# A residual stream kept with tokens on partitions, with down and output projections whose stationary operand is the activations

## The chip, the core and the metric

The kernel runs on one core of one Trainium2 chip. The metric is device time in microseconds (us) from the first to the last instruction of the program, with what lies around it; less is better. The time before is 2877.26 us, the median of two runs (2877.17 and 2877.34).

## What is computed

Two layers over 256 tokens of width 2048, in float32. Each layer adds to x half of a gated feed forward (FFN, inner width 4096), then a mixer, then half of a second FFN. The mixer of layer 0 is a gated delta net with pooling (GDN), that of layer 1 a latent attention (MLA) with 16 heads.

```
def swiglu(h, w_gate, w_up, w_down):
    return (jax.nn.silu(h @ w_gate) * (h @ w_up)) @ w_down
...
    for layer in range(DEPTH):
        x = x + 0.5 * swiglu(rms_norm(x, ffn1_norm[layer]), ...)
        h = rms_norm(x, mix_norm[layer])
        x = x + delta_pool_mixer(h, ...)  or  mla_mixer(h, ...)
        x = x + 0.5 * swiglu(rms_norm(x, ffn2_norm[layer]), ...)
```

So there are six norms, four down projections (4096 to 2048) and two output projections (2048 to 2048), `wgo` in GDN and `wmo` in MLA.

## The kernel before

**Precision.** Every large product is made from float32r parts. A weight piece of 1024 columns is split by `piece` (L163 to L169): ACT writes the rounded part `whi`, DVE writes the rest `wlo`. An activation tile is split in the same way into [128, 2, 256]: high part, then low part. Three of the four part products are kept: whi with high, whi with low, wlo with high.

**Layout.** x lies with features on partitions: 16 tiles of 128 features by 256 tokens. All large products have the weights as stationary side (128 x 128, loaded into the array) and the activations as moving side. In `mm3` the wide form is one product of whi with [high | low], 512 columns, and one of wlo with high, 256 columns, both into one PSUM bank of 128 features by 512. The narrow form (GDN's and MLA's input projections) is three products of 256 columns.

**Down projection.** For each of 16 feature tiles d: 32 K tiles of `g`, two products each; then DVE adds the two halves of the bank to x (`add_residual`, two operations of 256 columns), and `after(d)` does the norm's share for this tile: `feed_parts` splits x[d] times the gain into `xg[d]` (ACT, then DVE), `feed_squares` adds its square to `acc` (POOL, for the last two tiles ACT and DVE). Since `xg[d]` is already in the layout that the next product wants, PE has no work at the handoff. `project_out` does the same for the output projections, where the first two feature tiles share their steps so that late activations are waited for later.

**Norm factor.** After the first products of the next stage PE sums `acc` over partitions with a product of ones (`end_norm`, L321), and ACT and DVE make R, the factor of every token, from it.

**Weights.** SP loads 1 MB at a time into one of three `raw` buffers; there are four buffers each of `whi` and `wlo`. PSUM has six banks for streamed products and two for others in the FFNs, four and four in the mixers.

**Order.** Instructions are traced in the order in which PE is to run them; latency-bound chains (`Chains`) are traced in between by a clock of estimated PE time, and a scheduler places them on each engine. Each engine runs its own list in order.

**Start and end.** `warm_up` (L270) issues eight float32 products of zeros while the first loads are under way. The first gate and up tiles (`opening`) then go through K in quarters as x comes in. At the end `store` writes each feature tile of x from ACT's queue.

Of the kernel before, what the change touches and what calls it, by code (L numbers as in the profile page):

```python
# [9 lines left out]
F32 = mybir.dt.float32  # L10
# [8 lines left out]
P = 128  # L19
# [78 lines left out]
class Builder:  # L98
# [17 lines left out]
    def behind(self, inst, earlier):  # L116
        """inst issues after `earlier` on their engine."""
# [4 lines left out]
    def table(self, which, out, in_, func, **kw):  # L122
        """An activation that needs a table set; all of them issue in the order of the trace."""
# [12 lines left out]
    def banks(self, mm, aux):  # L136
        """The phase's PSUM: how many banks for the streamed products and how many for all others."""
# [10 lines left out]
    def split_hi_lo(self, dst, src, scale=None):  # L148
        """dst [P, 2, n] (float32r) = the two exact parts of src * scale."""
# [13 lines left out]
    def piece(self, raw, h):  # L163
        """The two exact parts of columns h : h + 1024 of a raw weight slab."""
# [6 lines left out]
    def weights(self, *aps):  # L171
        """Stream [P, L] weight slabs; yields (hi, lo) pieces [P, 1024]."""
# [15 lines left out]
    def gemm(self, ps, stream, acts, wide=True):  # L188
        """ps[:, :256] (+ ps[:, 256:] when wide) = W^T act over the K tiles in acts ([P, 2, 256] hi/lo)."""
# [25 lines left out]
    def squares(self, dst, src):  # L215
        """dst [P, 2, n] (float32r) = the two exact parts of src^2."""
# [6 lines left out]
    def total(self, out, which, sq):  # L223
        """out = the sums of sq over the partitions that `which` (float32r, 0 or 1) joins."""
# [3 lines left out]
    def rsqrt(self, out, ss, scale, newton, tag="rs"):  # L228
        """out = (ss * scale + EPS) ** -0.5, elementwise."""
# [18 lines left out]
    def token_major(self, r, out):  # L248
        """out [P, 2] = the row that all partitions of r [P, 256] hold, tokens on partitions."""
# [20 lines left out]
    def warm_up(self):  # L270
        """Products of zeros while the first loads are under way: TensorE's clock doubles after 3.4 us of work."""
        z = self.tmp([P, S], "res")
        self.nc.vector.memset(z, 0.0)
# [5 lines left out]
    def load_x(self, c):  # L279
        """A quarter of x and its part in the first norm."""  # L280
        t = self.xp.tile([P, 4, S], F32, tag=f"x{c}", name=f"x{c}")
        self.nc.sync.dma_start(t, self.i["x"][:, 4 * c : 4 * c + 4, :])
        self.x += [t[:, k, :] for k in range(4)]

    def load_rest(self):
        self.nc.sync.dma_start(self.ca, self.i["ca"])
        self.nc.scalar.copy(self.ones_r, self.ones)
        for d in range(KT):
            self.feed_squares(d, False)

    def begin_norm(self, gain):
        self.gain = gain
        self.xg = [None] * KT
        self.acc = self.tmp([P, S], "acc", 1)

    def feed_parts(self, d):
        """Splits x[d] * gain."""
        t = self.xp.tile([P, 2, S], F32R, tag=f"xg{d}", name=self.nm("xg"))
        self.split_hi_lo(t, self.x[d], self.gains[:, self.gain, d : d + 1])
        self.xg[d] = t  # L300

    def feed_squares(self, d, pool):
        """Adds x[d]^2 to the sum of squares."""
        nc = self.nc
        eng = nc.gpsimd if pool else nc.vector
# [819 lines left out]
```

## Time and profile before

| | before |
|---|---|
| median of the runs | 2877.26 us |
| profiled execution, span | 2874.8 us |
| PE busy | 2866.9 us, 17322 products |
| weight loads (PEld) busy | 2527.4 us |
| DVE / ACT / POOL busy | 1888.8 / 1439.9 / 200.3 us |
| DMA read | 507.74 MB |

The page gives for each engine the time in which an instruction of it was under way. PE's instructions overlap, so PE busy for the whole span does not say how fast it goes; for that one reads the distance between the starts of products in the timeline. The chain that ended last is the list of what the last instruction waited for, followed back to the start.

### The profile page before, as it was taken

How to read it: one execution, taken by the hardware profiler on the slowest of the kernel's cores; microseconds unless marked ns; L12 is line 12 of the kernel's file. 1: busy time of each engine (PE TensorE's matmuls, PEld its weight loads, DVE VectorE, ACT ScalarE, POOL GpSimd, SP SyncE). 2: the span in 40 equal slices, each digit the busy share in tenths (PEclk: the TensorE clock that was granted, in tenths of full speed). 3: DMA queues.
4: the chain of work that ended last, by engine and by line, in shares of the span. 5: the costliest groups of instructions: out<-in, count | busy, mean ns of one | idle time of the engine just before them, and what ended most of it. 6: DMA issues, size and time to landing. Idle time of an engine off the chain costs nothing.

```text
span 2874.8 us, 42334 instructions
## 1 busy us (share of the span) xinstructions
PE 2866.9 (100%) x17322; PEld 2527.4 (88%) x17322; DVE 1888.8 (66%) x2683; ACT 1439.9 (50%) x2146; POOL 200.3 (7%) x228
## 2 busy tenths in 40 slices
PE   9999999999999999999999999999999999999999
PEld 8888888899998888888888888888998888888888
DVE  7666666676787766666656666666777776666554
ACT  6444443475464544444345444544577454444433
POOL 0000011000003000001110000011122210000000
PEclk9999999999999999999999999999999999999999
DMA  6555555544245555555555555555533455555553
GB/s 247 183 188 190 183 184 189 187 147 164 88 162 191 189 183 185 190 185 183 189 190 179 188 190 185 183 189 189 183 125 112 151 185 191 185 185 187 196 195 137
DMA packets 77843, 512.70 MB, mean 178 GB/s; under 512 B 10833, under 2 KB 13649, under 8 KB 16849
## 3 DMA queue, kind: packets, MB, share of 16 engines
q1 hardware_dynamic: 74192, 506.81, 50.0%
q10 hardware_dynamic: 3456, 3.20, 0.3%
q8 instruction: 135, 2.21, 0.3%
q14 instruction: 60, 0.48, 0.1%
HBM read 507.74 MB, written 2.10 MB: 177 GB/s over the span
## 4 chain that ended last, share of the span: by engine, by line
PE 98%; issue 1%; DVE 0%; ACT 0%; POOL 0%; DMA 0%; SPq 0%; DVEq 0%; ACTq 0%; POOLq 0%
PE mm L186 93%; PE aux L186 4%; PE aux L641 0%; PE aux L957 0%; ACT whi L167 0%; DMA x<-in_x 0%; DVE wlo L168 0%; POOL osq L221 0%; PE aux L321 0%; ACT xg L155 0%; DVE y L485 0%; POOL sq L221 0%; PE aux L681 0%; DVE cb L627 0%; DVE tg L626 0%
## 5 line engine op out<-in xcount | busy, mean ns | idle before, releaser
L186 PE MATMUL mm<-xg,whi 128*128 128x512 f32 (+1 forms) x5664 | 1717.8, 367 | 0.9 <-ACT whi L167 0.9
L168 DVE TENSOR_TENSOR wlo<-raw,whi 128x1024 fp32r<-128x1024 f32 x960 | 1197.4, 1248 | 572.7 <-ACT whi L167 564.4
L167 ACT CAST whi<-raw 128x1024 fp32r<-128x1024 f32 x960 | 1007.8, 1050 | 799.8 <-PE mm L186 688.0
L186 PE MATMUL mm<-xg,wlo 128*128 128x256 f32 x4880 | 1330.2, 281 | 0.5 <-DVE wlo L168 0.5
L186 PEld LDWEIGHTS mm<-xg,whi 128*128 128x128 f32 x5664 | 997.7, 189 | 167.8 <-ACT whi L167 1.3
L186 PEld LDWEIGHTS mm<-xg,wlo 128*128 128x128 f32 x4880 | 923.2, 189 | 26.4 <-DVE wlo L168 1.0
L186 PE MATMUL mm<-g,whi 128*128 128x512 f32 x2048 | 719.1, 398 | 0.0
L186 PE MATMUL mm<-g,wlo 128*128 128x256 f32 x2048 | 564.7, 281 | 0.0
L186 PEld LDWEIGHTS mm<-g,whi 128*128 128x128 f32 x2048 | 380.8, 188 | 89.7
L186 PEld LDWEIGHTS mm<-g,wlo 128*128 128x128 f32 x2048 | 386.8, 189 | 6.0
L392 ACT COPY u<-mm 128x256 f32<-128x256 f32 x256 | 95.1, 372 | 465.4 <-PE mm L186 465.3
L393 DVE TENSOR_TENSOR t<-mm,u 128x256 f32<-128x256 f32 x256 | 108.7, 425 | 247.0 <-ACT u L392 246.9
L394 DVE TENSOR_TENSOR t<-t,R 128x256 f32<-128x256 f32 x256 | 108.6, 426 | 8.4
L312 POOL TENSOR_TENSOR acc<-acc,sq 128x256 f32<-128x256 f32 x65 | 100.1, 1539 | 5.1
L186 PE MATMUL mm<-o,whi 128*128 128x512 f32 x256 | 89.6, 395 | 0.0
L308 POOL TENSOR_TENSOR acc<-x 128x256 f32<-128x256 f32 x5 | 3.1, 613 | 1206.1 <-DVE x L333 1158.7
L156 DVE SCALAR_TENSOR_TENSOR xg<-x,gains,xg 128x256 fp32r<-128x256 f32 x96 | 76.3, 807 | 6.3 <-ACT xg L155 6.3
L152 ACT CAST g<-t 128x256 fp32r<-128x256 f32 x128 | 52.1, 407 | 56.5 <-DVE t L415 56.5
L308 POOL TENSOR_TENSOR sq<-x 128x256 f32<-128x256 f32 x65 | 44.5, 685 | 432.6 <-DVE x L333 356.1
L186 PE MATMUL mm<-o,wlo 128*128 128x256 f32 x256 | 69.3, 281 | 0.0
L332 DVE SCALAR_TENSOR_TENSOR res<-mm,x 128x256 f32<-128x256 f32 x64 | 27.2, 424 | 46.6 <-PE mm L186 46.6
L415 DVE TENSOR_TENSOR t<-t,t 128x256 f32<-128x256 f32 x128 | 54.5, 426 | 4.2
(256 smaller groups left out, 1757.9 us busy)
## 6 DMA issues: line engine op xcount, KB each, us to landing
raw<-in_w1d SPq DMA_DIRECT2D x64, 1024.0 KB, 5.0
raw<-in_w2g SPq DMA_DIRECT2D x64, 1024.0 KB, 4.8
raw<-in_w2u SPq DMA_DIRECT2D x64, 1024.0 KB, 4.8
raw<-in_w2d SPq DMA_DIRECT2D x64, 1024.0 KB, 4.9
raw<-in_w1g SPq DMA_DIRECT2D x62, 1024.0 KB, 4.8
raw<-in_w1u SPq DMA_DIRECT2D x62, 1024.0 KB, 4.9
raw<-in_wqk SPq DMA_DIRECT2D x16, 1024.0 KB, 4.8
raw<-in_wgo SPq DMA_DIRECT2D x16, 1024.0 KB, 4.8
```

The costliest lines, as they stand in the source:

```text
L152: nc.scalar.copy(dst[:, 0, :], src)
L156: nc.vector.scalar_tensor_tensor(dst[:, 1, :], src, scale, dst[:, 0, :].bitcast(F32), op0=ALU.mult, op1=ALU.subtract)
L167: self.nc.scalar.copy(hi, raw[:, h : h + 1024])
L168: self.nc.vector.tensor_tensor(lo, raw[:, h : h + 1024], hi.bitcast(F32), op=ALU.subtract)
L186: return self.nc.tensor.matmul(out, lhsT, rhs, start=start, stop=stop)
L308: eng.tensor_tensor(dst, self.x[d], self.x[d], op=ALU.mult)
L312: eng.tensor_tensor(self.acc, self.acc, dst, op=ALU.add)
L332: nc.vector.scalar_tensor_tensor(t, ps[:, S : 2 * S], 0.5, x, op0=ALU.mult, op1=ALU.add)
L392: nc.scalar.copy(u, ps[:, S : 2 * S])
L393: nc.vector.tensor_tensor(t, ps[:, 0:S], u, op=ALU.add)
L394: nc.vector.tensor_tensor(t, t, R, op=ALU.mult)
L415: nc.vector.tensor_tensor(tu, tu, tg, op=ALU.mult)
```

## The change

1. x lies with tokens on partitions: four tiles j of [128 tokens, 2 token blocks, 512 features]. The down weights `wd` and the output weights `wgo`, `wmo` are laid out in `wide_slabs`: four slabs of 512 output features, all K in each.
2. `project` replaces the down loop and `project_out`. For every j and K tile, and each of two token blocks t, it issues three products of 512 columns: the activation's 128 x 128 part is stationary, `whi` or `wlo` moves. Each j has two PSUM banks, and the residual is one DVE operation of 512 columns per bank.
3. At a handoff `feed_norm(j)` squares x on ACT with a sum per token (`accum_out`), turns x back by PE transposes (16 of 128 x 128 for each j), and splits the PSUM result into `xg`. After j = 3 `norm_factor` makes the factor r per token on [128, 2] and a diagonal `dg` of it; `end_norm` multiplies ones with `dg`, and ACT copies R.
4. The first x comes twice: `xf` as before for the first norm, and token-major x on POOL's queue. `store` writes two DMAs for each j from SP.
5. `warm_up` adds 64 products of zeros of several forms, with a [128, 2048] tile `zr` cleared by DVE.

```
-        for n in range(8):
-            self.nc.tensor.matmul(ps[:, 0:S], z[:, 0:P], z, start=n == 0, stop=n == 7)
+        for n in range(8):
+            nc.tensor.matmul(ps[:, 0:S], z[:, 0:P], z, start=n == 0, stop=n == 7)
...
+        row(zr[:, 0:512], 8)
+        row(zr[:, 0:512], 8, (a, b))
+        row(zb, 6, lhsT=zb[:, 0:P])
+        row(zr[:, 0:256], 8)
+        row(zr[:, 0:384], 6)
+        row(zr.rearrange("p (a c) -> p a c", a=2)[:, :, 0:256], 6)
+        row(zr[:, 0:1024].rearrange("p (c a) -> p c a", a=2)[:, :, 0], 6)
+        row(zr[:, 4:516], 6)
+        row(zr[:, 16:528], 6)
+        row(zr[:, None, 0:256].to_broadcast([P, 2, 256]), 6)
+        row(z, 4, lhsT=z[:, 0:P])
...
+    def feed_squares(self, j):
+        for t in range(2):
+            sq = self.tmp([P, 512], "sq", 1)
+            self.nc.scalar.activation(sq, self.x[j][:, t, :], AF.Square, accum_out=self.ss[:, t, j : j + 1])
+    def norm_factor(self):
+        nc = self.nc
+        tot = self.tmp([P, 2], "tot", 1)
+        nc.vector.tensor_reduce(tot, self.ss, axis=AX.X, op=ALU.add)
+        self.r2 = self.tmp([P, 2], "r2", 1)
+        self.rsqrt(self.r2, tot, 1.0 / D, True, "rt")
+        self.dg = self.tmp([P, 2, P], "dg", 1)
+        for t in range(2):
+            nc.vector.tensor_scalar(self.dg[:, t, :], self.ident, self.r2[:, t : t + 1], None, op0=ALU.mult)
+    def feed_norm(self, j):
+        yield 1.2 * LAG
+        self.feed_squares(j)
+        if j == 3:
+            self.norm_factor()
+        x = self.x[j]
+        for h in range(2):
+            ps = self.psum("aux")
+            for n in range(2):
+                for t in range(2):
+                    c = (2 * h + n) * P
+                    self.nc.tensor.transpose(ps[:, (2 * n + t) * P : (2 * n + t + 1) * P], x[:, t, c : c + P], self.ident)
+                    self.ch.clock += P / 2.4
+            for n in range(2):
+                self.feed_part(4 * j + 2 * h + n, ps[:, n * S : n * S + S])
+            if h == 0:
+                yield 0.5 * LAG
...
+    def project(self, slabs, acts, half, after):
+        K = len(acts)
+        st = self.weights(*[slabs[j] for j in range(4)])
+        blk = [slice(0, P), slice(P, 2 * P)]
+        for j in range(4):
+            ps = [self.psum("mm") for _ in range(2)]
+            for k in range(K):
+                if k % 2 == 0:
+                    piece = next(st)
+                hi, lo = (w[:, 512 * (k % 2) : 512 * (k % 2) + 512] for w in piece)
+                self.ch.wait(lambda: acts[k] is not None)
+                a = acts[k]
+                for t in range(2):
+                    self.mm(ps[t], a[:, 0, blk[t]], hi, start=k == 0, stop=False)
+                    self.mm(ps[t], a[:, 0, blk[t]], lo, start=False, stop=False)
+                    self.last_mm = self.mm(ps[t], a[:, 1, blk[t]], hi, start=False, stop=k == K - 1)
+                self.ch.poll()
+            for t in range(2):
+                x = self.x[j][:, t, :]
+                if half:
+                    self.nc.vector.scalar_tensor_tensor(x, ps[t], 0.5, x, op0=ALU.mult, op1=ALU.add)
+                else:
+                    self.nc.vector.tensor_tensor(x, ps[t], x, op=ALU.add)
+            after(j)
```

On PE, at the start of the first down projection, the order before was (mm is a PSUM bank, g an activation tile of the FFN; a name's number is that of its buffer):

```order
L186 MATMUL mm_3446<-g_398,whi_3449 128x512
L186 MATMUL mm_3446<-g_398,wlo_3450 128x256
L186 MATMUL mm_3446<-g_413,whi_3449 128x512
L186 MATMUL mm_3446<-g_413,wlo_3450 128x256
L186 MATMUL mm_3446<-g_514,whi_3449 128x512
```

and at the same place it is now:

```order
L186 MATMUL mm_3505<-whi_3509,g_457 128x512
L186 MATMUL mm_3505<-wlo_3510,g_457 128x512
L186 MATMUL mm_3505<-whi_3509,g_457 128x512
L186 MATMUL mm_3506<-whi_3509,g_457 128x512
L186 MATMUL mm_3506<-wlo_3510,g_457 128x512
L186 MATMUL mm_3506<-whi_3509,g_457 128x512
```

Two products of 512 and 256 columns for each K tile and 128 features have become six of 512 for each K tile and 512 features.

On PE, at the start of the program, these rows now stand between the branch and the first real product (aux_80 takes the eight products of before; zr and res are the zero tiles); the 8 MATMULs of the third piece stand alternately in two banks and are left out, as are five pairs that repeat:

```order
L281 MATMUL aux_80<-res_76 128x256 x8
L288 MATMUL mm_89<-zr_78 128x512 x9
...
L288 LDWEIGHTS res_76
L288 MATMUL mm_89<-res_76 128x512
...
L288 MATMUL mm_89<-zr_78 128x256 x8
L288 MATMUL mm_89<-zr_78 128x384 x6
L288 MATMUL mm_89<-zr_78 128x512 x30
L288 MATMUL mm_89<-res_76 128x256 x4
L186 MATMUL mm_167<-xg_172,whi_186 128x512
```

Before, the first real product stood right behind the first of these rows.

On PE, at the handoff from the first down projection to GDN's first unit, the last j's transposes (x_405) stand eight and ten K tiles into the unit (rows between are left out):

```order
L186 MATMUL mm_4387<-whi_4670,g_3502 128x512
L186 MATMUL mm_4721<-xg_3821,whi_4724 128x256 x2
...
L361 MATMUL aux_4770<-ca,x_405 128x128 x4
...
L186 MATMUL mm_4721<-xg_4428,wlo_4785 128x256
L361 MATMUL aux_4794<-ca,x_405 128x128 x4
...
L186 MATMUL mm_4721<-xg_4775,wlo_4785 128x256
...
L186 MATMUL mm_4721<-xg_4802,wlo_4785 128x256
L371 MATMUL aux_4823<-dg_4767,ca 128x256
```

and on ACT, at the same handoff, the copies of their results stand behind loads of GDN's parameters:

```order
L484 DMA par_4692<-in_gpar 128x144
L489 DMA cb_4694<-in_wab 128x256
L494 DMA cg_4699<-in_cg 128x1024
L500 CAST identb_4704<-ca 128x128
L491 CAST h_779_4696<-cb_4694 128x16x16
L336 ACTIVATE sq_4749,ss_3781<-x_405 128x512
L155 ACTIVATE xg_4775<-aux_4770,gains 128x256
L336 ACTIVATE sq_4751,ss_3781<-x_405 128x512
L498 CAST mask_781_4701<-cg_4699 128x128
L498 CAST mask_781_4701<-cg_4699 128x128
L131 ACTIVATE rtl_4756<-tot_4753,eps 128x2
L155 ACTIVATE xg_4778<-aux_4770,gains 128x256
```

Before, x went into `xg` without PE, and no product stood in PE's list for it.

## Rows read from the trace of the kernel before

**Rows 1.** Page: busy time of engines, granted clock in 40 slices, chain.

```profile
PE 2866.9 (100%) x17322; PEld 2527.4 (88%) x17322; DVE 1888.8 (66%) x2683; ACT 1439.9 (50%) x2146; POOL 200.3 (7%) x228
PEclk9999999999999999999999999999999999999999
PE 98%; issue 1%; DVE 0%; ACT 0%; POOL 0%; DMA 0%; SPq 0%; DVEq 0%; ACTq 0%; POOLq 0%
```

**Rows 2.** Windows: the four down projections, GDN's output projection.

```profile
core 0: us, PE busy (x) PEld busy (x) DVE busy (x) ACT busy (x) POOL busy (x), PEclk, DMA share, GB/s
370.60:551.30 180.70, 180.70 (x1025) 156.74 (x1025) 110.35 (x114) 74.38 (x82) 29.40 (x27) 1.00 0.54 187
...
2690.10:2870.80 180.70, 180.70 (x1025) 156.74 (x1024) 89.01 (x95) 64.73 (x63) 0.00 (x0) 1.00 0.52 177
862.70:952.30 89.60, 89.60 (x518) 78.51 (x517) 70.57 (x86) 42.30 (x52) 29.64 (x27) 1.00 0.53 189
```

**Rows 3.** Timeline of PE, MLA's output projection: start us, duration us, instruction.

```profile
2289.65 0.39 PE L186 MATMUL mm<-o,whi 128*128 128x512 f32 x1
...
2291.05 0.39 PE L186 MATMUL mm<-o,whi 128*128 128x512 f32 x1
```

**Rows 4.** Timeline of PE, MLA's v projection (weights move, activations are stationary).

```profile
2126.30 0.39 PE L186 MATMUL mm<-whi,kv 128*128 128x256 f32 x2
...
2127.32 0.28 PE L186 MATMUL mm<-whi,kv 128*128 128x256 f32 x1
```

**Rows 5.** Timeline of PE, wide products in an FFN.

```profile
1200.32 0.40 PE L186 MATMUL mm<-xg,whi 128*128 128x512 f32 x1
1200.56 0.28 PE L186 MATMUL mm<-xg,wlo 128*128 128x256 f32 x1
1200.67 0.40 PE L186 MATMUL mm<-xg,whi 128*128 128x512 f32 x1
```

**Rows 6.** Timeline of PE, four transposes among narrow products in GDN.

```profile
768.24 0.28 PE L186 MATMUL mm<-xg,wlo 128*128 128x256 f32 x1
768.36 0.60 PE L681 MATMUL aux<-ca,y 128*128 128x128 f32 x4
768.72 0.48 PE L186 MATMUL mm<-xg,whi 128*128 128x256 f32 x2
769.03 0.28 PE L186 MATMUL mm<-xg,wlo 128*128 128x256 f32 x1
```

**Rows 7.** Timeline of PE, the start of the program.

```profile
1.22 5.90 PE L277 MATMUL aux<-res 128*128 128x256 f32 x16 [1.22 <-DVE res L273]
8.03 0.73 PE L186 MATMUL mm<-xg,whi 128*128 128x512 f32 x2 [0.91 <-ACT whi L167]
9.29 0.39 PE L186 MATMUL mm<-xg,wlo 128*128 128x256 f32 x1 [0.52 <-DVE wlo L168]
```

**Rows 8.** Groups by line and form: busy us, mean ns, idle before.

```profile
L321 PE MATMUL aux<-acc,ca 128*128 128x256 f32 x12 | 3.6, 379 | 0.0
L252 PE MATMUL aux<-ca,R 128*128 128x1 f32 x4 | 0.5, 230 | 0.0
L168 DVE TENSOR_TENSOR wlo<-raw,whi 128x1024 fp32r<-128x1024 f32 x960 | 1197.4, 1248 | 572.7 <-ACT whi L167 564.4
L332 DVE SCALAR_TENSOR_TENSOR res<-mm,x 128x256 f32<-128x256 f32 x64 | 27.2, 424 | 46.6 <-PE mm L186 46.6
```

**Rows 9.** Timeline of all engines, the end of the program.

```profile
2871.15 0.42 DVE L332 SCALAR_TENSOR_TENSOR res<-mm,x 128x256 f32<-128x256 f32 x1 [8.99 <-PE mm L186]
2871.61 0.42 DVE L333 SCALAR_TENSOR_TENSOR x<-mm,res 128x256 f32<-128x256 f32 x1
2872.07 0.34 ACTq L427 DMA_DIRECT2D out<-x  x1
```

**Rows 10.** Issues and landings of the loads of `in_w1d`.

```profile
L178 SPq DMA_DIRECT2D raw<-in_w1d x64: 327/328/328, 351.2 to 2013.7; - x64
DMA to landing us min/median/max: 4.8/5.0/7.2
```

More of the change, by code (lines that the diff above doesn't have):

```diff
@@ L276, in warm_up, with row, load_xf @@
         for n in range(8):
-            self.nc.tensor.matmul(ps[:, 0:S], z[:, 0:P], z, start=n == 0, stop=n == 7)
[L279 to L283, printed above, removed]
-    def load_rest(self):
[L286 to L289, printed above, removed]
+            nc.tensor.matmul(ps[:, 0:S], z[:, 0:P], z, start=n == 0, stop=n == 7)
+        a, b = self.psum("mm"), self.psum("mm")
+        w = zr[:, 1024:1152]
+        def row(rhs, count, outs=(a,), lhsT=w):
+            size = int(np.prod(rhs.shape[1:]))
+            for n in range(count):
+                nc.tensor.matmul(outs[n % len(outs)][:, 0:size], lhsT, rhs, start=True, stop=True)
+        row(zr[:, 0:512], 8)
[9 more added lines that the diff above has]
+        row(z, 4, lhsT=z[:, 0:P])
+    def load_xf(self, c):
+        t = self.xp.tile([P, 4, S], F32, tag=f"x{c}", name=f"xf{c}")
+        self.nc.sync.dma_start(t, self.i["xf"][:, 4 * c : 4 * c + 4, :])
+        for k in range(4):
+            self.feed_part(4 * c + k, t[:, k, :])
+    def load_rest(self):
+        nc = self.nc
+        nc.sync.dma_start(self.ca, self.i["ca"])
+        nc.scalar.copy(self.ones_r, self.ones)
+        for j in range(4):
+            t = self.xp.tile([P, 2, 512], F32, tag=f"x{j}", name=f"x{j}")
+            nc.gpsimd.dma_start(t, self.i["x"][:, j])
+            self.x.append(t)
+        for j in range(4):
+            self.feed_squares(j)
+        self.norm_factor()
     def begin_norm(self, gain):
@@ L373, in opening @@
                         nc.sync.dma_start(dst, src[0:2, :, k4].rearrange("f p k -> p f k"))
-                    for k in range(4):
-                        self.feed_parts(4 * c + k)
                     for w in range(2):
@@ L418, in ffn, with store @@
                 g.append(gt)
-            st = self.weights(*[wd[d] for d in range(KT)])
-            for d in range(KT):
-                ps = self.psum("mm")
-                self.gemm(ps, st, g)
-                self.add_residual(d, ps, True)
-                after(d)
-    def store(self, d):
-        self.nc.scalar.dma_start(self.out[:, d, :], self.x[d])
+            self.project(wd, g, True, after)
+    def store(self, j):
+        for t in range(2):
+            self.nc.sync.dma_start(self.out[:, j, t, :], self.x[j][:, t, :])
 def gdn(b, after):
@@ L503, in gates @@
             yield 2 * LAG
-            Rt = b.token_major(R, tl([P, 2], "Rt"))
+            Rt = b.r2
             ps = b.psum("aux")
@@ L1004, in mla @@
         acts = LateList(lambda k: o[k], MH)
-        b.project_out(i["wmo"], acts, after)
+        b.project(i["wmo"], acts, False, after)
 def layers(b):
@@ L1033, in slabs, with wide_slabs @@
     return w.reshape(K // P, P, N // P, P).transpose(2, 1, 0, 3).reshape(N // P, P, K)
+def wide_slabs(w):
+    K = w.shape[0]
+    return w.reshape(K // P, P, 4, 512).transpose(2, 1, 0, 3).reshape(4, P, 4 * K)
 def columns(v, n):
@@ L1067, in prepare @@
         for s, k in (("g", "gate"), ("u", "up"), ("d", "down")):
-            n[f"w{f}{s}"] = np.stack([slabs(a[f"ffn{f}_w_{k}"][l]) for l in range(2)])
+            lay = wide_slabs if s == "d" else slabs
+            n[f"w{f}{s}"] = np.stack([lay(a[f"ffn{f}_w_{k}"][l]) for l in range(2)])
     w = a["hyb_w_in"][0]
@@ L1084, in prepare @@
     w = a["hyb_w_out"][0]
-    n["wgo"] = slabs(np.concatenate([w[:1024]] + [w[1024 + P * c : 1152 + P * c] for c in POOL_ORDER], 0))
+    n["wgo"] = wide_slabs(np.concatenate([w[:1024]] + [w[1024 + P * c : 1152 + P * c] for c in POOL_ORDER], 0))
     w = a["mla_w_in"][0]
@@ L1118 @@
            for k, v in arrays.items()}
-    out = nc.dram_tensor("out", (P, KT, S), F32, kind="ExternalOutput").ap()
+    out = nc.dram_tensor("out", (P, 4, 2, 512), F32, kind="ExternalOutput").ap()
     with tile.TileContext(nc) as tc:
@@ L1123 @@
     y = r.results[0]["out"]
[L1124 removed]
+    return np.ascontiguousarray(y.transpose(2, 0, 1, 3).reshape(1, S, D))
```

73 lines of the change are left out of this document (20 added, 53 removed).

## The prediction

> **What bounds the kernel now.** I read the page first: PE is busy for 2866.9 of the 2874.8 us, the chain that ended last is PE's for 98%, and the granted clock is at full speed (2.4 GHz) in every slice [rows 1]. DVE and ACT, at 66% and 50%, are not the bound. So the time is what PE's instructions cost, one behind another, plus a start and an end. A busy PE does not tell its speed, so I next read distances between starts. A wide pair (512 and 256 columns) takes 0.24 + 0.11 = 0.35 us [rows 5]. At one column per cycle of 2.4 GHz, 768 columns would take 0.320 us, so some 10% is lost even where PE never waits. The windows give the stages that the change rewrites: each down projection, 512 such pairs, takes 180.7 us (four times the same), 0.353 us a pair, and GDN's output projection 89.6 us for 256 pairs [rows 2]. MLA's takes 0.350 a pair (four pairs from 2289.65 to 2291.05 [rows 3]), 256 x 0.350 = 89.6 us of its own products; other work stands in between and stays. Together 4 x 180.7 + 2 x 89.6 = 902.0 us of the span.
>
> **The change, part by part.**
>
> *Products of the projections.* The number of columns is the same: before 512 x 768 = 393,216 for a down projection, now 4 x 32 x 6 = 768 products of 512 columns, 393,216 again. Only the price of a column can change: 256 pairs or 512 pairs become 384 or 768 equal products, 4 x 768 + 2 x 384 = 3840 in all. No row has such a product of 512 columns. Bounds: not under 512 / 2.4 = 213 ns, a column per cycle at the granted clock [rows 1], which makes 3840 x 0.213 = 819 us, 83 less than now; and not over the dearest 512 column product of before, 0.24 us [rows 5], which makes 922 us, 20 more. The nearest row in kind is MLA's v projection: there too the split weights move, an activation is stationary and is used twice in a row. Nine of its products go from 2126.30 to 2127.32 [rows 4], 113.3 ns for 256 columns. I take twice that, 226.7 ns for 512, since it agrees in operands and order and differs only in length: 3840 x 0.2267 = 870.5 us, **-31.5 us**. Were part of the loss a fixed cost for a product rather than for a column, 512 would cost less than twice 256; if it is the length that makes it dear, more. I keep 220 to 232 ns as this case's own width (-57 to -11 us).
>
> The Trainium skill, TensorE: Matmul & The Clock Gate, section "Wait — 56ns, not 53.3ns?", gives a warm product N / 2.4 + 2.5 ns, so 215.7 ns for 512 columns. The rows disagree with it for products of this kind (0.24 us in rows 5); by the rule the term would be 3840 x 0.2157 - 902 = -74 us. It stands below as a rival, priced there from the clock alone.
>
> *Transposes.* Five handoffs (the first norm is fed from `xf`, the last has none) times 4 x 8 transposes each: 160. In GDN four of them, with one product of 256 before and two behind, fill 768.24 to 769.03, 0.79 us; three products of 0.12 leave 0.43 us for four [rows 6]. So 40 x 0.43 = **+17.2 us**, all on PE, where nothing hides it.
>
> The Trainium skill, TensorE: Matmul & The Clock Gate, section "Part 4: PE-mode transpose", tells of about 275 ns for one in a kernel's context, which would make 160 x 0.275 = 44 us, 27 more than by the row. This trace has 109 ns for one; that decides here.
>
> *Warm-up.* Before, PE ends the eight zero products at 1.22 + 5.90 = 7.12 us, and real products run without a gap from 9.29 us; counting the two products that ran before that gap (about 0.47 us), the opening starts in effect at 8.8 us [rows 7]. Now 46 float32r and 6 bf16 products of 512, 8 of 256 and 6 of 384 columns follow: 30,976 columns. At the v projection's 0.443 ns a column that is 13.7 us (12.9 at the clock, 14.5 at the dearest row). Four float32 products of 256 are added; six such took 3.6 us busy [rows 8], 0.6 each, and overlap, so about 2 us. PE is then free at 7.1 + 15.7 = 22.8 us. By then x, the first weights and their parts lie ready, as they did at 9.3 us before plus DVE's clearing of `zr` (a few us); so the start is later by 22.8 - 8.8 = **+14.0 us** (12.5 to 16). Before, the cover of the warm-up was that PE waited anyway; only 1.7 us of such cover is left.
>
> *Handoffs.* Before, `xg` was ready without PE. Now the last quarter of x goes residual, transpose, ACT, DVE. The last residual costs DVE 424 ns at 256 columns and the split 1248 ns at 1024 [rows 8], so about 0.7 us at 512; the transposes stand eight K tiles into the next product (some 2.8 us), which hides it, except at MLA's end. What is late next is ACT: at GDN's start its copies of the transposed tiles stand behind parameter loads and casts that wait for them, and PE waits for those copies four K tiles later, with all of the unit behind it. The scheduler has put products of the next unit in between. I count 1 us for each of GDN's and MLA's start and 1 us for the other three: **+3 us** (0 to 10). The factor's products stay (one ones product, L321), R is now a copy, and GDN's `token_major` falls away, -0.5 us [rows 8].
>
> *Off the path.* POOL's squares and sums (200 us busy [rows 1]) go, and DVE's residual shrinks; ACT gets eight squares of 512 for each norm. In a down projection DVE is busy 110 and ACT 74 of 181 us [rows 2], so neither gain nor cost shows.
>
> *Loads.* The same bytes in 1 MB loads, with rows of a slab farther apart. A load is used in 24 products x 0.227 = 5.4 us, against 2 x 8 x 0.353 = 5.6 us before. It lands in 5.0 us [rows 10], with three buffers. No change.
>
> *End.* Before, the last two residual operations of 0.42 us and a store of 128 KB follow PE [rows 9]. Now one operation of 0.7 us stands behind the last product, and a store of twice the size: 0 (up to 1 us more).
>
> Sum: -31.5 + 17.2 + 14.0 + 3.0 - 0.5 = **+2.2 us** on a span of 2874.8, so 2877.0; the median of the runs is 2.5 us above this span, so **2879.5 us**. All but the first term are +33.7 us.
>
> **The rivals.**
>
> *A. The products run near a column per cycle* (213 to 220 ns). For: nothing in their order makes PE wait, and there are a quarter fewer weight loads, if these are what costs. Against: every long float32r product in the trace is above that. At 213: -83 + 33.7 = -49, 2828 us; at 216: 2838; at 220: 2854. Even this is within 2%.
>
> *B. Slower: length, not the role of the operands, sets the price,* so that 512 columns cost 232 to 241 ns as now. For: the dearest long product has 0.24 us [rows 5]. Against: the v projection. At 236: 906 us, +4 + 33.7 = +38, 2915 us. The layout then gains nothing and pays for transposes and warm-up. It is slower by over 2% (57.5 us) from 241.1 ns on, where the projections cost 23.8 us more than now; that is the dearest row of the trace for every product.
>
> *C. The handoffs stall.* Each waits for an ACT queue blocked by a load, or for `dg`, for 5 to 10 us: 5 x 8 = 40 in place of 3, 2917 us. Against: x waits for nothing else that is slow, and PE has products of the next unit.
>
> *D. The change doesn't do what it says:* the wide slabs' loads land late and PE waits for weights. It would need landings of well over the 5.4 us of use for three buffers; 5.0 stands against it. At 1 us of wait for each of the 160 loads (32 for a down projection, 16 for an output projection) it would be 3040 us.
>
> **How the numbers follow.** The likeliest case (220 to 232 ns, 2854 to 2901 us) 0.55; A 0.15; B 0.22; C 0.06; D 0.02. The predicted time is the likeliest case's 2879.5. The range reaches to 2840 into A (leaving out about a third of it) and to 2918 into B and C (leaving out a fifth of B, half of C, and D): about 0.15 is outside. Two per cent is 57.5 us, about what a measurement of this kernel can tell from no change. Faster than 2819.7 needs a column in less than a cycle or a stall that I do not see in the kernel before: 0.03. Slower than 2934.8 is B's dearest end, or C or D at their worst: 0.07. Within: 0.90.
>
> **What would show each step right or wrong.** In the trace after, a down projection of 174 us, with 227 ns from start to start; 160 transposes in groups of four that widen the distance between their neighbours by 0.43 us; the first real product at about 22.8 us; POOL near idle; no idle time of PE over 1 us at handoffs. The prediction is wrong if a 512 column product with moving weights costs 213 or 240 ns, or if PE waits for ACT, for `dg`, or for a landing.

## The result, and the profile after

| | before | after |
|---|---|---|
| median of the runs | 2877.26 us | 2904.93 us (2904.86 to 2904.99) |
| profiled execution, span | 2874.8 us | 2903.2 us |

The ratio is 1.0096, 95% interval 1.0067 to 1.0125: slower by 27.7 us, within the 2%. Forecast were 2879.5 us, with 2840 to 2918 around it, so the time lies inside the whole range, but 4 us above the likeliest case's own 2854 to 2901.

The page after, to be laid beside [rows 1]: engines, granted clock in 40 slices, the chain's shares, and the loads of the first down weights (KB each, median us to landing).

```profile
PE 2895.9 (100%) x16272; PEld 2492.8 (86%) x16272; DVE 1776.9 (61%) x2532; ACT 1462.9 (50%) x2222; POOL 57.5 (2%) x97
PEclk9999999999999999999999999999999999999999
PE 98%; issue 1%; ACT 0%; DVE 0%; POOL 0%; DMA 0%; ACTq 0%; POOLq 0%; DVEq 0%
raw<-in_w1d SPq DMA_DIRECT2D x64, 1024.0 KB, 4.8
```

PE is still the bound, at full clock, with a thousand products fewer. POOL has lost its norm work, DVE 112 us; neither moved the end. The wide slabs land in 4.8 us, against 5.0 before [rows 10].

Windows of the kernel after: the first and the last down projection, GDN's output projection and MLA's (columns as in [rows 2]).

```profile
386.40:568.10 181.70, 181.70 (x793) 146.30 (x792) 89.32 (x87) 76.83 (x90) 0.00 (x0) 1.00 0.54 186
...
2719.90:2898.90 179.00, 179.00 (x768) 143.81 (x768) 80.14 (x72) 64.61 (x63) 0.00 (x0) 1.00 0.51 176
880.70:974.60 93.90, 93.90 (x422) 76.10 (x421) 52.41 (x60) 44.72 (x60) 0.00 (x0) 1.00 0.52 183
2250.50:2356.60 106.10, 106.10 (x486) 83.84 (x485) 59.14 (x88) 52.48 (x90) 1.88 (x2) 1.00 0.43 155
```

The two output projections before, from the first of their products to the first of the next stage (the window in [rows 2] ends 1.6 us before GDN's does):

```profile
862.80:953.90 91.10, 91.10 (x526) 79.81 (x525) 71.80 (x87) 42.31 (x52) 29.64 (x27) 1.00 0.54 192
2223.90:2328.20 104.30, 104.30 (x590) 87.86 (x590) 77.80 (x114) 49.91 (x82) 31.60 (x29) 1.00 0.46 165
```

Each tile j takes 8 transposes (the section on the change says 16), so 32 for a handoff and 160 in all, as the trace has them. A down projection with the 24 of its first three j inside takes 181.7 us (the three that have them agree within 0.1), the last, without any, 179.0. So 768 products cost 233.1 ns each, where 226.7 were forecast and where the same work took 180.7 us before. The timeline of PE says it directly: nine products lie between these two starts.

```profile
2799.99 0.39 PE L186 MATMUL mm<-wlo,g 128*128 128x512 f32 x1
...
2802.09 0.40 PE L186 MATMUL mm<-wlo,g 128*128 128x512 f32 x1
```

2.10 us over nine is 233.3 ns.

Four transposes in the first down projection, on PE's timeline:

```profile
435.19 0.39 PE L186 MATMUL mm<-whi,g 128*128 128x512 f32 x1
435.41 0.60 PE L361 MATMUL aux<-ca,x 128*128 128x128 f32 x4
435.77 0.48 PE L186 MATMUL mm<-whi,g 128*128 128x512 f32 x1
436.09 0.39 PE L186 MATMUL mm<-wlo,g 128*128 128x512 f32 x1
```

From 435.19 to 436.09 pass 0.90 us with two products of 0.233 in them, so 0.43 us for the four, as [rows 6] had it.

The start: a window that holds five of the products whose moving columns stand two apart (time, PE busy, granted clock, DMA share, GB/s; the count takes in one that reaches over its edge), then the bf16 products, the end of the zero products and the first real one on PE's timeline.

```profile
16.48:18.75 2.27, 2.27 (x6) 1.00 1.03 405
```

```profile
11.37 1.47 PE L288 MATMUL mm<-res 128*128 128x512 bf16 x6
...
22.91 1.89 PE L288 MATMUL mm<-res 128*128 128x256 f32 x8
24.45 0.91 PE L186 MATMUL mm<-xg,whi 128*128 128x512 f32 x2
```

The added products are 70 (16, 6, 44 and 4, where a float32 product has two records), not 64 as the section on the change says; the forecast counted 70. The first real product stands at 24.45 us where 22.8 was forecast, and from there to the first down projection PE never waits. Most of the 1.65 us are the six products with a step of two columns: 453 ns each (2.27 us for five) where 227 had been counted for all of 512.

Where the 28.4 us between the two spans come from, by the starts of the stages: the first down projection begins at 386.43 us, before at 370.65, so the opening costs 15.8 us; the products of the down projections give back 4 x (180.7 - 179.0) = 6.8; the output projections, less 2.6 us for the 24 transposes of each, take 91.3 us where they took 91.1 (GDN) and 103.5 where they took 104.3 (MLA), other work included, so they give back 0.6; 160 transposes take 17.3. That makes 25.7, and 2.7 us are left for the handoffs, R and the end, a remainder that also takes up the rounding of the others.

### The profile page after: what moved, and what is told of

Read it like the earlier page. It is cut to its first block, busy times and chain, and to the rows that moved or that the text cites. A ratio compares the mean times of both kernels' runs of the same rounds, so it can differ in the third digit from the quotient of the medians.

```text
span 2903.2 us, 39987 instructions
## 1 busy us (share of the span) xinstructions
PE 2895.9 (100%) x16272; PEld 2492.8 (86%) x16272; DVE 1776.9 (61%) x2532; ACT 1462.9 (50%) x2222; POOL 57.5 (2%) x97
## 3 DMA queue, kind: packets, MB, share of 16 engines
q8 instruction: 127, 2.08, 0.3%
## 4 chain that ended last, share of the span: by engine, by line
PE 98%; issue 1%; ACT 0%; DVE 0%; POOL 0%; DMA 0%; ACTq 0%; POOLq 0%; DVEq 0%
PE mm L186 92%; PE aux L186 4%; PE mm L288 1%; PE aux L361 1%; PE aux L281 0%; PE aux L681 0%; PE aux L997 0%; ACT sq L336 0%; POOL osq L221 0%; DMA cb<-in_wab 0%; PE aux L371 0%; ACT L126 0%; ACT whi L167 0%; ACT xg L155 0%; DVE x L398 0%
## 5 line engine op out<-in xcount | busy, mean ns | idle before, releaser
L186 PEld LDWEIGHTS mm<-xg,wlo 128*128 128x128 f32 x4880 | 923.2, 189 | 25.7
L186 PE MATMUL mm<-whi,g 128*128 128x512 f32 x2048 | 648.5, 396 | 0.0
L186 PEld LDWEIGHTS mm<-whi,g 128*128 128x128 f32 x2048 | 384.0, 187 | 92.9
L186 PE MATMUL mm<-wlo,g 128*128 128x512 f32 x1024 | 404.5, 395 | 0.0
L186 PEld LDWEIGHTS mm<-wlo,g 128*128 128x128 f32 x1024 | 192.0, 188 | 46.0
L186 PE MATMUL mm<-whi,o 128*128 128x512 f32 x256 | 84.2, 399 | 0.0
L221 POOL TENSOR_TENSOR sq<-sqf,sq 128x256 fp32r<-128x256 f32 x49 | 45.4, 932 | 1337.2 <-ACT sq L220 1324.1
L186 PEld LDWEIGHTS mm<-whi,o 128*128 128x128 f32 x256 | 47.9, 187 | 11.1 <-DVE o L153 0.2
L131 ACT ACTIVATE t<-t 128x256 f32<-128x256 f32 x128 | 53.5, 418 | 5.8 <-DVE t L438 5.4
L153 DVE TENSOR_TENSOR g<-t,g 128x256 fp32r<-128x256 f32 x128 | 53.5, 418 | 0.0
L186 PE MATMUL mm<-wlo,o 128*128 128x512 f32 x128 | 50.5, 395 | 0.0
```

The costliest lines, as they stand in the source:

```text
L131: a = nc.scalar.activation(out, in_, func, **kw)
L153: nc.vector.tensor_tensor(dst[:, 1, :], src, dst[:, 0, :].bitcast(F32), op=ALU.subtract)
L186: return self.nc.tensor.matmul(out, lhsT, rhs, start=start, stop=stop)
L221: nc.gpsimd.tensor_tensor(dst[:, 1, :], sq, dst[:, 0, :].bitcast(F32), op=ALU.subtract)
```

## The experiments

All edits are to the changed kernel unless it is said otherwise. The kernel before ran beside each of them, with medians of 2876.95 to 2877.33 us, so medians are compared directly. Line numbers in a row are those of that experiment's own kernel.

### The transposes, twice

```
-            for n in range(2):
+            for n in (0, 1, 0, 1):
                 for t in range(2):
                     c = (2 * h + n) * P
```

> The changed kernel with each group of four transposes issued twice into the same place, so 160 more (the result is the same). Theory: a transpose costs TensorE 0.109 us and nothing hides it, so the time goes up by 160 x 0.109 = 17.4 us: about 2922 us. Rival: transposes partly fill time in which TensorE would wait anyway (handoffs), so under 9 us: 2905 to 2914 us. Second rival: the chain from the transposes to the next stage's activations is what PE waits for, so that their doubling costs more than 25 us.

Measured: 2922.25 us, 17.3 more than the changed kernel, as the theory had it; both rivals fall. The term of +17.2 was right and nothing hides it. The groups by line, of the changed kernel and of this one, show a trap (line, instruction, count | busy us, mean ns of one):

```profile
L361 PE MATMUL aux<-ca,x 128*128 128x128 f32 x160 | 24.2, 272 | 0.0
```

```profile
L361 PE MATMUL aux<-ca,x 128*128 128x128 f32 x320 | 41.6, 273 | 0.0
```

One transpose is under way for 272 ns in both, yet 160 more cost 17.3 us, 108 ns each. The Trainium skill's 275 ns for one (TensorE: Matmul & The Clock Gate, "Part 4: PE-mode transpose") agrees with this length, 272 ns; the length is no price for transposes that follow each other.

### The opening: no added zero products, then x loaded late

The first kernel keeps only the eight zero products of before.

```
-        row(zr[:, 0:512], 8)
-        row(zr[:, 0:512], 8, (a, b))
...
-        row(z, 4, lhsT=z[:, 0:P])
```

> The changed kernel with the eight zero products of before as its only warm-up (zr and the 64 added products left out). Theory: the added products stand alone on TensorE's path, so the kernel gets faster by the 15 to 16 us by which its first real product starts later now (24.45 us against 8.03, less the gap that stood behind the first products before): about 2889 us, ratio to the kernel before 1.004. Rival: the opening is bound by something that comes with the change too (x on another queue, xf, the first parts), so that taking the products away gives back under 5 us: 2900 us or more, and an idle TensorE between the zero products and the first real one.

Measured: 2896.85 us, only 8.1 less. The first down projection begins at 377.08 us, 6.4 later than before the change, so much of the opening's 15.8 us stayed; of the 9.3 that came back, MLA's stage lost 1.1 again, for a reason that was not looked for. The result lies between theory and rival, and the rival's reason is in the trace. The first real product is at 7.72 us, and later PE waits. Its timeline, ACT's, and PE's windows (time, PE busy, granted clock, DMA share, GB/s):

```profile
31.24 0.50 PE L186 MATMUL mm<-xg,whi 128*128 128x512 f32 x1 [1.60 <-ACT whi L167]
32.50 0.38 PE L186 MATMUL mm<-xg,wlo 128*128 128x256 f32 x1 [0.76 <-DVE wlo L168]
```

```profile
29.53 0.63 ACT L314 ACTIVATE sq<-x 128x512 f32<-128x512 f32 x1 [4.59 <-DMA x<-in_x]
30.07 0.19 ACT L314 ACTIVATION_READ_ACCUMULATOR sq<-x 128x1 f32 x1
30.16 1.03 ACT L167 CAST whi<-raw 128x1024 fp32r<-128x1024 f32 x1
```

```profile
32.00:33.00 1.00, 0.50 (x3) 1.00 0.00 0
33.00:34.00 1.00, 1.00 (x7) 0.88 0.52 115
34.00:36.00 2.00, 2.00 (x8) 0.50 0.86 352
...
37.00:38.00 1.00, 0.55 (x3) 0.91 0.00 0
```

ACT runs its list in order. A square of token-major x waits 4.59 us for its load, the rounding of the next weights stands behind it, and PE waits for that. After the two waits the clock fell to 0.50, which is 1.2 GHz, until about 37 us. The second kernel takes the first norm from `xf`, as before, and loads token-major x only five units later, from SP's queue in place of POOL's:

```
-            nc.gpsimd.dma_start(t, self.i["x"][:, j])
-        for j in range(4):
-            self.feed_squares(j)
-        self.norm_factor()
+        for d in range(KT):
+            dst = self.acc if d == 0 else self.gp.tile([P, S], F32, tag="sqx", bufs=2, name=self.nm("sqx"))
+            nc.scalar.square(dst, self.xf[d])
+            if d > 0:
+                nc.vector.tensor_tensor(self.acc, self.acc, dst, op=ALU.add)
...
+                if start and f == 5:
+                    self.load_x()
```

> The changed kernel with the eight zero products of before as its only warm-up, and with the first norm as before: its squares are taken from xf (ACT, added up by DVE), the factor comes from a product of ones with their sum, and token-major x, which only the first down projection's residual needs, is loaded by SP five units later instead of at once. Theory: without the added zero products the opening is bound by the 2 MB of x that come with it and by ACT's squares that wait for them ahead of the weights' rounding (TensorE stood still for 1.60 us behind ACT at 31.24 us and the clock fell to 0.50); with that gone the 16 us come back in full: first down projection at about 370 us as before, 2889 us. Rival: the waits only move (ACT and DVE have more to do for squares of 256 columns), 2894 us or more.

Measured: 2890.03 us, another 6.8 less. The first down projection begins where it did before the change (370.65 us):

```profile
370.97 0.39 PE L186 MATMUL mm<-whi,g 128*128 128x512 f32 x1
```

So the opening had two costs, one behind the other: the zero products, and the 2 MB of x with the squares that wait for it. While the zero products stood, they hid the wait for x; without them it came out. The reverse, x late with the zero products kept, was not run, nor were the three parts of this edit (squares, queue, time of the load) run one by one. What is left of the change, 2890.0 - 2877.3 = 12.7 us, is about 17.3 + 2.7 - 7.4.

### The price of a product: its length?

Every 512 column product of the projections is cut into two of 256, with operands and order as in MLA's v projection, on which the forecast rested.

```
-                    self.mm(ps[t], a[:, 0, blk[t]], hi, start=k == 0, stop=False)
-                    self.mm(ps[t], a[:, 0, blk[t]], lo, start=False, stop=False)
...
+                    for n in range(2):
+                        c = slice(S * n, S * n + S)
+                        self.mm(ps[t][:, c], a[:, 0, blk[t]], hi[:, c], start=k == 0 and n == 0, stop=False)
+                        self.mm(ps[t][:, c], a[:, 0, blk[t]], lo[:, c], start=False, stop=False)
...
```

> The changed kernel with every 512 column product of the down and output projections cut into two of 256 columns (first the three of one half, then the three of the other), as MLA's v projection has them; the same columns, twice the products. Theory: only the number of columns counts, at 0.456 ns each as now (233.3 ns for 512), and the cheap stretch of nine at 113.3 was a stretch and no price: 3840 x 2 x 116.7 = 896 us, the same time within 8 us, 2897 to 2913 us. Rival 1: the length is what costs, and products of 256 take 113.3 ns as the prediction had it: 870 us, 25 us faster, 2880 us. Rival 2: they take the 120 ns of the narrow products in the input projections: 922 us, 26 us slower, 2930 us.

Measured: 2903.87 us. The last down projection, as a window:

```profile
2718.50:2897.50 179.00, 179.00 (x1535) 178.96 (x1535) 80.15 (x72) 64.85 (x63) 0.00 (x0) 1.00 0.51 177
```

179.0 us again, with twice the products: 116.6 ns for 256 columns. The length is not what costs: rival 1 of this run and rival 2 fall, and rival B's reason ("length, not the role of the operands") falls with it, though its price came true.

### Where the tiles start

Three kernels ask whether the address sets the price. The first moves all tiles of the kernel before by 96 bytes of a partition:

```
-        self.eps = self.cst.tile([P, 1], F32, name="eps")
+        self.eps = self.cst.tile([P, 32], F32, name="eps")[:, 0:1]
```

> The kernel before with the one-float constant eps taking 128 bytes of each partition in place of 32: all weight and activation tiles then start at a multiple of 128 bytes instead of 32 bytes behind one; nothing else changes. Theory: where a tile starts sets the price of a float32r product (pairs on U and h, that start 64 bytes behind a multiple of 128, take 348 ns, those on xg and g 353.3), so the wide pairs fall to 350 ns or less: 3.3 ns for each of some 5100 wide pairs, 17 us or more, 2860 us or less. Rival: the price does not depend on the address: 353.3 ns a pair as before and the same time within 3 us, 2874 to 2880 us.

Measured: 2877.44 us, no change (ratio 1.0001, interval 0.9992 to 1.0011). A common shift changed nothing, so the theory falls. The next has rows of products in the place of the added warm-up (`w` and `zr` start 32 bytes behind a multiple of 128):

```
+        for n in range(18):
+            nc.tensor.matmul(A, w, zr[:, 8:520], start=True, stop=True)
+        for n in range(18):
+            nc.tensor.matmul(A, w, zr[:, 24:536], start=True, stop=True)
+        for n in range(18):
+            nc.tensor.matmul(A, zr[:, 1048:1176], zr[:, 24:536], start=True, stop=True)
...
```

> The changed kernel with 13 rows of 18 float32r products in place of the added warm-up, of 512 columns but for three rows of 256: zeros with one stationary tile from an address 32 bytes behind a multiple of 128, the same 64 and 128 bytes behind, the stationary tile at a multiple of 128 too, all 18 added up in one bank, two stationary tiles in turn, two moving tiles in turn, both as in a down projection; then 256 columns at both addresses and in that pattern; then real weights, one stationary tile, and the pattern of a down projection. Theory 1, the pattern (stationary and moving tile change, one bank takes the sum) sets the 233 ns: 226 to 227 ns in the plain rows, 233 in the rows with the pattern. Theory 2, real data set it: 227 ns in all rows of zeros, 233 in the last two. Theory 3, what else runs beside the products sets it (DVE, ACT and loads): 226 to 227 ns in all rows.

PE's timeline; each row holds 18 products, and the distance to the next row over 18 is the price:

```profile
7.21 4.48 PE L289 MATMUL mm<-zr 128*128 128x512 f32 x18
11.53 4.36 PE L291 MATMUL mm<-zr 128*128 128x512 f32 x18
15.73 4.35 PE L293 MATMUL mm<-zr 128*128 128x512 f32 x18
19.92 4.30 PE L295 MATMUL mm<-zr 128*128 128x512 f32 x18
...
28.17 4.24 PE L299 MATMUL mm<-zr 128*128 128x512 f32 x18
32.25 4.24 PE L301 MATMUL mm<-zr 128*128 128x512 f32 x18
```

The rows that start at 11.53 and 15.73 us, moving tile 64 and 128 bytes behind, stationary at 32: 233.3 and 232.8 ns. The row at 28.17, both at 32: 4.08 us over 18, 226.7. The row at 19.92, both at 128, takes 229.4 as a whole: its first nine products have a mean of 232, its last are at 226.7. Neither two stationary tiles in turn, nor two moving ones, nor a sum in one bank, nor real weights raised the price: theories 1 and 2 fall. Theory 3 has most rows for it, but not the two at 233. These stood beside heavy loads, so loads have to be ruled out; the first row does it. Both its tiles are at 32, and its last eight products are this window (PE busy, granted clock, DMA share, GB/s; the count takes in two that reach over an edge):

```profile
9.71:11.53 1.82, 1.82 (x10) 1.00 0.99 333
```

1.82 us over eight is 227 ns, with the DMA engines as busy as in the row behind it, which never came under 230. What is left between the two rows is where the tiles start against each other.

No row of a trace shows an address; the offsets here are worked out from the sizes of the tiles in the kernel. In the changed kernel `whi` and `wlo` start 32 bytes behind a multiple of 128, `g`, `U`, `h`, `nx` and `y` at one, and `o` 96 behind. Two small tiles made longer move them all to 32:

```
-        tot = self.tmp([P, 2], "tot", 1)
+        tot = self.tmp([P, 10], "tot", 1)[:, 0:2]
...
-                    lat["kvt"] = b.token_major(r, tl([P, 2], "rt"))
+                    lat["kvt"] = b.token_major(r, tl([P, 10], "rt")[:, 0:2])
```

> The changed kernel with two small tiles (tot, and rt in MLA) made 32 bytes of a partition longer, so that the activations of the down and output projections (g, U, h, nx, y, o) start 32 bytes behind a multiple of 128, as the weight parts whi and wlo do; until now g, U, h, nx and y started at a multiple of 128 and o 96 behind it. Theory: a 512 column product takes 226.7 ns where stationary and moving tile have the same offset and 233.3 where they have not, as in the rows of zeros (rows at 32 and 32, and at 0 and 0, settle at 226.7; rows at 64 and 32, and at 0 and 32, stay at 233.3): 3840 x 6.67 = 25.6 us faster, 2879 us, which is where the prediction had it. Rival: in the stream something else sets 233.3 (other traffic, the changing tiles; the wide pairs of before have the same offsets on both sides and yet take 353.3 ns): no change, 2902 to 2907 us.

Measured: 2884.20 us, 20.7 us less, from two paddings of 32 bytes. The last down projection and GDN's output projection as windows, and the nine products of above on PE's timeline:

```profile
2704.40:2878.40 174.00, 174.00 (x769) 144.03 (x768) 80.15 (x72) 65.03 (x63) 0.00 (x0) 1.00 0.52 182
875.30:968.80 93.50, 93.50 (x422) 76.01 (x422) 52.40 (x60) 44.67 (x60) 0.00 (x0) 1.00 0.52 184
```

```profile
2799.90 0.39 PE L186 MATMUL mm<-wlo,g 128*128 128x512 f32 x1
...
2801.94 0.39 PE L186 MATMUL mm<-wlo,g 128*128 128x512 f32 x1
```

174.0 us and 226.7 ns: the forecast's numbers, to the digit. But only in the down projections, 4 x 4.9 us; the output projections, with equal offsets too now, gained 0.4 us here and 0.1 in MLA, where the theory had 2.6 for each. So the offset is a cause, and not the whole of it.

### All offsets, and kernels that use them

48 rows of zero products, each run once, with offsets of whi and of wlo against the activations through 0, 32, 64 and 96 bytes:

```
+        offs = [(dw, dl) for dw in (0, 8, 16, 24) for dl in (0, 8, 16, 24)]
+        for dw, dl in offs:
+            for n in range(30):
+                k = n % 2
+                wh, wl = zr[:, 1024 + dw + P * k : 1152 + dw + P * k], zr[:, 1536 + dl + P * k : 1664 + dl + P * k]
+                nc.tensor.matmul(A, wh, zr[:, 512 * k : 512 * k + 512], start=n == 0, stop=n == 29)
+                if n < 29:
+                    nc.tensor.matmul(H, wl, zr[:, 512 * k : 512 * k + 256], start=False, stop=False)
...
```

> The changed kernel with 48 rows of zero products in place of the added warm-up, nothing else beside them: 16 rows of 30 wide pairs (512 and 256 columns, the weights stationary), 16 of 24 narrow triples (three of 256), 16 of 20 triples as in a down projection (activations stationary, 512 columns); in each 16 the offsets of the two weight parts against the activations are 0, 32, 64 and 96 bytes, all combinations. Theory: the offsets set the price: with equal offsets the cheap one (wide pair 346.7 ns, triple of 512 680 ns), with others 353.3 and 700. Rival: the price depends on how a row begins and not on the offsets: rows of one kind differ without order, or all agree.

The rows left out of the edit are three of 256 columns, and three of 512 with the activation stationary. Windows of PE over five rows: 30 products of 512 and 29 of 256 columns at offsets 0 and 96, then at 32 and 96; then 20 triples as in a down projection, at 0 and 0, at 0 and 32, at 32 and 32 (time, PE busy, the count with those that reach over an edge, granted clock, DMA share, GB/s).

```profile
38.50:48.92 10.42, 10.42 (x60) 1.00 0.01 2
...
80.16:90.45 10.29, 10.29 (x61) 1.00 0.01 2
...
309.76:323.37 13.61, 13.61 (x63) 1.00 0.01 1
323.37:337.27 13.90, 13.90 (x62) 1.00 0.00 0
379.01:393.01 14.00, 14.00 (x62) 1.00 0.00 0
```

13.61, 13.90 and 14.00 us over 20 are 680, 695 and 700 ns a triple. Read from the later part of each row, a triple took 680 ns at equal offsets, 687 to 700 at all others; that part of the theory held. A wide pair took 346 to 347 ns at equal offsets and at six other pairs of offsets, 349 to 353 at the rest; a narrow triple 353 to 357, and 360 at equal offsets. So there is an order, but not one rule, "equal is cheap". Two kernels test it in the layout of before, with unused gaps of 32 to 96 bytes between the tiles:

```
+    def gap(self, pool, n, tag):
+        if n and tag not in self.gapped:
+            self.gapped.add(tag)
+            pool.tile([P, n], F32, tag=tag, bufs=1, name=tag)
...
+        self.gap(self.wp, 16, "gap_raw")
         return self.wp.tile([P, 2048], F32, tag="raw", bufs=3, name=self.nm("raw"))
...
+        self.gap(self.wp, 24, "gap_lo")
         lo = self.wp.tile([P, 1024], F32R, tag="wlo", bufs=4, name=self.nm("wlo"))
```

The second kernel has 24 for `gap_raw` and no `gap_lo`; in both a gap ahead of the next pool, and longer tiles in GDN and MLA, hold the activations at one offset.

> The kernel before with unused gaps between its tiles, so that whi starts 64 and wlo 32 bytes behind the offset of every activation tile (xg, g, U, h, nx, y, o), all modulo 128 bytes; until now xg, g, nx, y, whi and wlo had one offset. In the rows of zeros a wide pair with these offsets took 346.3 ns and a narrow triple 353.4, with equal offsets 346.7 and 360.0. Theory: these prices hold in the stream too, where wide pairs take 353.3 now: 6656 wide pairs x 7.0 = 46 us and 784 narrow triples x 6.6 = 5 us, about 2826 us. Rival: in the stream the pairs stay at 353.3 whatever the offsets (the row at equal offsets had 346.7 and the kernel has 353.3): 2872 to 2880 us.

Measured: 2858.94 us, ratio 0.9937 (0.9919 to 0.9954). Faster, but by 18 us and not by 51. The first down projection, 512 wide pairs, as a window (180.7 us before):

```profile
368.40:547.80 179.40, 179.40 (x1026) 157.20 (x1025) 110.31 (x114) 74.41 (x82) 29.38 (x27) 1.00 0.55 189
```

In the stream a wide pair takes some 350 ns, not the 346.3 of the rows of zeros.

> The same with both weight parts 96 bytes behind the activations' offset (modulo 128). The rows of zeros had 346.7 ns for a wide pair and 356.1 for a narrow triple; pairs on U and h in the kernel before stood at that offset and took 348. Theory: 6656 x 6.6 = 44 us and 784 x 3.9 = 3 us less, about 2830 us. Rival: no change, 2872 to 2880 us.

Measured: 2838.10 us, ratio 0.9864 (0.9848 to 0.9880), 39 us less, 8 short of the 47 that were expected. An FFN's gate and up products and a down projection as windows (361.9 and 180.7 us before), and PE's timeline, with six pairs between the two starts:

```profile
942.10:1298.10 356.00, 356.00 (x2051) 1.00 0.54 189
```

```profile
1298.10:1475.90 177.80, 177.80 (x1025) 157.18 (x1025) 110.33 (x115) 74.39 (x82) 29.39 (x27) 1.00 0.55 191
```

```profile
1200.23 0.39 PE L194 MATMUL mm<-xg,whi 128*128 128x512 f32 x1
...
1202.31 0.39 PE L194 MATMUL mm<-xg,whi 128*128 128x512 f32 x1
```

2.08 us over six is 346.7 ns a pair, and by the windows the mean is 347 to 348; before, a pair of the down projections took 353 [rows 2]. Last, the changed kernel with all of it: opening mended, activations of the projections at the offset of the weights, `xg` so that the weights stand 96 bytes behind it.

```
+        self.gap(self.xp, 8, "gap_x")
+        self.gap(self.wp, 24, "gap_raw")
```

The edits of the late x and of `tot` and `rt` stand as above.

> The changed kernel with its opening mended (eight zero products, first norm from xf, x loaded late), with the activations of the down and output projections at the offset of the weight parts, and with xg so placed that the weight parts stand 96 bytes behind its offset. Theory: the three add up: 2904.9 - 14.9 - 20.7 = 2869 us from the first two, and if the offset counts for wide pairs too, 4096 of them in gate and up x 6.6 ns = 27 us less, 2842 us. Rival: the wide pairs keep their 353.3 ns, 2866 to 2872 us.

Measured: 2841.87 us, ratio 0.9877 (0.9860 to 0.9895), where 2842 was expected. The sum came out, but not all its parts: by the starts of the stages the four gate and up stages gave 23.8 us, not 27, and GDN's input products, whose price the sum left alone, gave 4.0. With their tiles well placed both layouts beat the kernel before, the old one by 39 us and the new one by 35. Between them 3.8 us are left, 0.13%.

## Why the prediction was right, and where it was not

**The time.** "Within 2%" held, and the sum's signs held: products down, transposes and opening up. The sum came out 25 us low, and one term is the cause. (The likeliest case ends at 2900 us by the forecast's own formula for 232 ns, not at 2901.)

**Products: -31.5 forecast, -7.4 measured.** The step that failed is "I take twice that, 226.7 ns", from nine products of MLA's v projection [rows 4]. The bounds were sound and the way was right; the row was one stretch taken for a price. Another stretch of the same projection, in the same trace of before:

```profile
2142.77 0.28 PE L186 MATMUL mm<-whi,kv 128*128 128x256 f32 x1
...
2144.78 0.28 PE L186 MATMUL mm<-whi,kv 128*128 128x256 f32 x1
```

17 products in 2.01 us, 118.2 ns, twice which is 236. Both prices stood in the trace. The mean over all stretches of that projection is 116 ns (171 distances between neighbours, two of over 200 ns left out), twice which is 232, and the stretches run from 226 to 236, where the forecast kept 220 to 232. With 233.3 ns the forecast's own formula gives 3840 x 0.2333 - 902.0 + 33.7 = +27.6, 2904.9 us, the measured time. To the digit this is luck: the opening cost 1.8 us more than its term, the products gave back 1.3 more than this, and the median lies 1.7 us above the span, not 2.5. That is rival B's price (0.22) for a reason that B did not give: not the length, but, in the down projections, where the stationary and the moving tile start against each other. With the tiles moved these alone give 4 x (174.0 - 180.7) = -26.8, close to the -31.5. That the output projections stayed near 233 ns is not explained. The Trainium skill's N / 2.4 + 2.5 ns (TensorE: Matmul & The Clock Gate, "Wait — 56ns, not 53.3ns?"), 215.7 ns for 512 columns, was rightly not taken: no float32r product of 512 columns settled below 226.7. The warm-up's bf16 products agree with it: six of them fill 1.47 us and the last is under way for 0.38, so five distances take 1.09 us, 218 ns each.

**Transposes: +17.2 forecast, 17.3 measured.** Read from a stretch between neighbours, not from an instruction's length.

**Warm-up: +14.0 forecast (12.5 to 16), 15.8 measured.** The path was right: PE is busy with zero products to the end, and x and the weights lie ready then, as the forecast said, since PE has no wait in the opening. The 1.35 us for the step of two columns were not foreseen. Nor was the second cost behind the first: x comes twice, and without the zero products that holds the opening up by 6.4 us.

**Handoffs, R and end: +2.5 forecast, 2.7 left over.** Apart from the start, the longest wait that PE has in the kernel after is 0.8 us. Rival C did not come, nor D: 4.8 us to a landing.

**Left open.** What it is that costs the 6.7 ns; why wide pairs at equal offsets take 346.7 ns in a row of zeros and 353.3 in the kernel before; why equal offsets helped the down projections and not the output projections (at the offset that `o` had, 64 bytes, a row of zeros took 686.7 ns a triple, and the stream 700). MLA's v projection has both prices, 113.3 and 118.2 ns, although the offsets of its tiles, worked out in the same way, are the same in both stretches, so the offset cannot be the only condition. The runs show that moving tiles against each other by 32 to 96 bytes changes the price. They show no rule that gives it.

## What to carry to other kernels

Price an operation by the mean over all its stretches in the trace, and take the spread of the stretches as the width; the new place need not be in the state of the cheapest stretch. When an operation on the bounding engine has two prices, try padding that moves its operands against each other before the layout is blamed or praised: here this was worth more (39 us) than the whole change. And a cost that hides behind another is not gone: take away the first and measure what is left.

## What the runs showed of the hardware

- A float32r product of 512 columns took 233.3 ns in the down projections, and 226.7 once its stationary and its moving tile started at the same offset modulo 128 bytes; in rows of zeros the mean was 226.7 at equal offsets and 229 to 233 at others. The output projections stayed near 233 at equal offsets. A wide pair in the stream took 353 ns, and 347 to 348 with the weights 96 bytes behind the activations. Moving all tiles together changed nothing (2877.44 us).
- A row of zero products at equal offsets could take its first nine at a mean of 232 ns before it settled at 226.7.
- Moving columns two floats apart cost 453 ns for 512, twice the 227 of columns side by side.
- A transpose of 128 x 128 is under way for 272 ns and costs 108 in a stream (160 more cost 17.3 us).
- In the kernel whose opening stalled, PE's clock was granted at 0.50 after waits of 1.60 and 0.76 us, and was back at full speed within about 4 us.
